# A small pool opened early and first place for the first pair's first tile in two SwiGLU networks of a decoder layer; the second network's first weights written down earlier

## The chip, the cores and the metric

The kernel runs on one core of one Trainium2 chip. The metric is the device time of one execution in microseconds (us). TensorE is the matmul engine, VectorE (DVE) and ScalarE (ACT) and GpSimd (POOL) do the elementwise work, and SyncE's queue (SP) issues most of the transfers.

## The reference

One decoder layer for 1024 prompt tokens and 8 x 4 sample tokens, 1056 in all, with model width 1024:

```
h = rms_norm(x) * (1 + scale) + shift
x = x + 0.5 * gate * swiglu(h)          # first network, D_FF = 2816
h = rms_norm(x) * (1 + scale) + shift
x = x + gate * (concat(gdn(h), mla(h)) @ w_out)      # the mixer
h = rms_norm(x) * (1 + scale) + shift
x = x + 0.5 * gate * swiglu(h)          # second network
...
def swiglu_ffn(h, wi, wo):
    gate, up = jnp.split(h @ wi, 2, axis=-1)
    return (jax.nn.silu(gate) * up) @ wo
```

Shift, scale and gate come from a conditioning vector per sequence (ada_w). All is in fp32.

## The kernel before, in words

**Data.** The 1056 tokens are four blocks of 264 (BW), features on partitions. Blocks 0 and 1 are the first pair (p = 0), blocks 2 and 3 the second. An fp32 product is made of three matmuls of rounded high and low halves (`mm3`, lines 127 to 129); `halve` (369 and 370) makes such halves: a cast on ScalarE, a subtraction on VectorE or GpSimd.

**Up projection.** `ffn_up` goes over 22 tiles of 128 features. Each tile and pair is a 2 x 2 product in Strassen's manner: seven products (PRODUCTS) of one form of the input (B11, T3, T2, B21, T1, T4, B22) with one form of the weights (A11, S3, S2, A12, S1, A22, S4), 12 matmuls each, summed in three PSUM banks X, Y, Z of that pair. `ffn_weights` makes the weight forms from two loads of 512 KB, g and u. `ffn_pair` writes the products and what takes them out of the banks: after B11 a copy s1 (487), after T2 the sums u2 and u3 (476), after T1 and T4 the two halves of cc, after B21 and B22 the Silu sg, at the end cc = sg * cc and its store (502). A bank is written again only after it has been taken out: B21 adds to X after s1, T1 needs Y after u2, T4 adds to Z after u3, B22 adds to Y after cc's half. Tile 0 uses the order B11, B21, T3, T2, T1, T4, B22 and writes the first pair in whole, then the second.

**Input forms.** `norm_squares` sums the squares of a block on ScalarE (nsq, 312) and VectorE or GpSimd (nacc, 315 and 319). `norm_sums` sums over partitions on TensorE (ss, 334) and takes the inverse root in nine small operations on VectorE (336 and 707 to 711). `norm_rows` spreads the root over the partitions on TensorE (rb, 347). `chain` then scales (354, 359, 361, 365), forms the differences (405) and halves the seven forms of a pair. Block 0 and 2 give B11 and B21; the rest of a pair's forms need its second block.

**Around the change.** In the first network the four chains run after the first conditioning products. In the second, `mixer_out` writes the output product: for two pairs of blocks, eight column tiles of w_out, 24 matmuls for each block and tile; the last two column tiles of the second pair are loaded and split by `split` (108 and 111) and multiplied block by block, so that block 2 is finished and normed before block 3. `then` starts a block's chain and is stepped on between products.

**Order of the work.** A planner takes the program as written, with a rank for each instruction from its place. Whenever an engine is free in the planner's own time line, it gives it the ready instruction of the lowest rank; the result is a fixed order for each engine's queue, which the chip keeps. `high_priority(n)` moves instructions n places ahead, `later(n)` n places back (LATE holds these numbers). Memory is a stack of pools; a tile of a pool that lies over an older pool is ordered only after the last use of the older one. The up projection's pool (t1, t2) lies over the norm's pool (tn, tn2) and over the residents x0 to x3, which also stage the chains of blocks 2 and 3. Its banks X, Y, Z lie over those of the output products.

**Weight buffers.** `wsp` has eight buffers of 4 KB per partition for halves of weights, `wraw` three for raw weights. The slots hi0 to hi3 and lo0 to lo3 hold the halves of the mixer's output and later the forms.

Of the kernel before, what the change touches and what calls it, by code (L numbers as in the profile page):

```python
# [8 lines left out]
F32 = mybir.dt.float32  # L9
# [8 lines left out]
P = 128  # L18
# [46 lines left out]
AHEAD = 1500  # L65


LATE = (100, 150, 110, 30, 110)


def f(ap):
# [13 lines left out]
class Kernel:  # L85
# [218 lines left out]
    def norm_squares(self, b, tp, k=0, n=KT, eng=None):  # L304

        nc = self.nc
        x = self.xb[b]
        eng = eng or nc.gpsimd
        for k in range(k, k + n, 2):
            m = min(n, 2)  # L310
            sq = tp.tile([P, 2, BW], F32, tag="nsq", name="nsq", bufs=2)
            nc.scalar.activation(sq[:, :m], x[:, k:k + m, :], AF.Square)
            if k == 0:
                self.nacc[b] = acc = tp.tile([P, BW], F32, tag="nacc", name="nacc", bufs=NB)
                eng.tensor_tensor(out=acc, in0=sq[:, 0], in1=sq[:, 1], op=ALU.add)
            else:
                acc = self.nacc[b]
                for j in range(m):
                    eng.tensor_tensor(out=acc, in0=acc, in1=sq[:, j], op=ALU.add)
# [5 lines left out]
    def norm_sums(self, blocks, tp, ps, late=0):  # L325

        nc = self.nc
        W = BW // 4
        ss = ps.tile([P, 512], F32, tag="C", name="ss")
        n = 4 * len(blocks)  # L330
        for at, b in enumerate(blocks):
            with self.later(late):
                for q in range(4):
                    nc.tensor.matmul(ss[:W, 4 * at + q:4 * at + q + 1], self.nacc[b][:, q * W:(q + 1) * W], self.ones, start=True, stop=True)
        v, r, t = (tp.tile([W, 4 * NB], F32, tag=n, name=n, bufs=3)[:, 0:n_] for n, n_ in (("nv", n), ("nr", n), ("nq", n)))
        nc.vector.tensor_scalar(v, ss[:W, 0:n], 1.0 / D, EPS, ALU.mult, ALU.add)
        self.rsqrt(r, v, t)
        for at, b in enumerate(blocks):
            self.nr[b] = r[:, 4 * at:4 * at + 4]

# [128 lines left out]
        part("S4", A12, nc.vector)  # L469
        return W  # L470

    def ffn_pair(self, p, W, dst, tp, ps, products):

        nc = self.nc
        T = lambda n: tp.tile([P, self.ffn_tiles[n][0]], F32, tag=f"{n}{p}", name=n, bufs=self.ffn_tiles[n][1])
        tt = lambda out, a, b, op=ALU.add: nc.vector.tensor_tensor(out=out, in0=a, in1=b, op=op)
        sg, cc = T("sg"), T("cc")
        B, F = {}, self.forms[p]
        for x, w, bank, add in products:
            if not add:  # L480
                B[bank] = ps.tile([P, 512], F32, tag=f"{bank}{p}", name="p" + bank)[:, 0:BW]
            for k in range(4):
                self.mm3(B[bank], W[w][:, 0, k], W[w][:, 1, k], F[x][:, 0, k], F[x][:, 1, k], k == 0 and not add, k == 3 and (add or x == "T2"),
                         skip_group_check=True)
            if x == "B11":
                s1 = T("s1")
                nc.scalar.copy(s1, B["X"])
            elif x == "T2":
                u2, u3 = T("u2"), T("u3")
                tt(u2, s1, B["Y"])  # L490
                tt(u3, u2, B["Z"])
            elif x == "B21":
                nc.scalar.activation(sg[:, :BW], B["X"], AF.Silu)
            elif x == "T1":
                tt(cc[:, BW:], u3, B["Y"])
            elif x == "T4":
                tt(cc[:, :BW], u2, B["Z"])
            elif x == "B22":
                tt(u3, u2, B["Y"])
                nc.scalar.activation(sg[:, BW:], u3, AF.Silu)  # L500
                tt(cc, sg, cc, ALU.mult)
                nc.sync.dma_start(out=dst[:, 2 * BW * p:2 * BW * p + 2 * BW], in_=cc)
            yield

    def ffn_up(self, wi, tp, ps, hook=lambda us: None, first=None):


        nf = wi.shape[1] // 2 // P

        self.ffn_tiles = {"cc": (2 * BW, 2), "sg": (2 * BW, 1), "u3": (BW, 1), "u2": (BW, 1), "s1": (BW, 1)}  # L510
        for p in range(2):
            for n, (w, bufs) in self.ffn_tiles.items():
                tp.tile([P, w], F32, tag=f"{n}{p}", name=n, bufs=bufs)
        for ff in range(nf):
            W = first if first and ff == 0 else self.ffn_weights(wi, ff, tp)
            order = PRODUCTS if ff else (PRODUCTS[0], PRODUCTS[3], *PRODUCTS[1:3], *PRODUCTS[4:])
            pairs = [self.ffn_pair(p, W, self.act_d[ff], tp, ps, order) for p in range(2)]
            for g in pairs if ff in (0, nf - 1) else [zip(*pairs)]:
                for _ in g:
                    hook(1.45 if g in pairs else 2.9)  # L520

    def ffn_down(self, wo, mgate, tp, ap, ps, each, load):

# [158 lines left out]
    def hook(self):  # L682

        done = object()
        for g in list(self.active):
            if next(g, done) is done:
                self.active.remove(g)
# [1369 lines left out]
                    for _ in smp:  # L2057
                        pass

    def mixer_out(self, tp, tn, ps, then):  # L2060


        nc, wo = self.nc, self.i["w_out"][0]
        parts = [self.mix_split(b) for b in range(NB)]

        def product(b, d, w):
            po = ps.tile([P, 512], F32, tag="B", name="po")
            for k in range(KT):
                self.mm3(po[:, :BW], w[0][:, k, :], w[1][:, k, :], parts[b][0][:, k, :], parts[b][1][:, k, :], k == 0, k == KT - 1)
            self.residual(b, d, 5, po, tp)  # L2070
        load = lambda d: self.split(self.load_cols(wo, d * P, P), (KT, P))
        side = iter(())
        for h in range(2):
            pair = (2 * h, 2 * h + 1)
            for d in range(KT - 2 * h):
                w = load(d)
                for b in pair:
                    product(b, d, w)
                    if d % 2:
                        self.norm_squares(b, tn, d - 1, 2, nc.gpsimd)  # L2080
                    next(side, None)
            if h == 0:
                self.norm_sums(pair, tn, ps)
                side = then(0, then(1, iter(())))
        ws = [load(d) for d in range(KT - 2, KT)]
        for b in pair:
            for n, w in enumerate(ws):
                product(b, KT - 2 + n, w)
                next(side, None)
                self.norm_squares(b, tn, KT - 2 + n, 1, nc.vector)  # L2090
            self.norm_sums([b], tn, ps, LATE[2] if b % 2 else 0)
            side = then(b, side)
        for _ in side:
            pass
# [19 lines left out]
def body(tc, ins, outs):  # L2114
# [15 lines left out]
    def pool(name, **kw):  # L2130
        return tc.tile_pool(reuse_waits="tile", name=name, bufs=1, **kw)

    with k.ctx:
        k.setup()
        k.dram()
        with k.weights():
            with k.extra():
                with k.residents(), ExitStack() as pse, pool("tn") as tn, pool("t0") as tp:
                    ps = banks(pse, "ps0", **DOWN)
                    k.small_vectors(ps, "C")  # L2140
# [13 lines left out]
                with ExitStack() as pse, pool("t1") as tp, pool("tk") as tk:  # L2154
                    ps = banks(pse, "ps1", **UP)

                    def background():
                        k.key_tables(tk, ps, "C")
                        yield from k.ada(2, 1, tk, ps, "C")
                        for m in (3, 5, 7):  # L2160
                            yield from k.ada(m, 2, tk, ps, "C")
                        raw = k.bcast_load(tk, ins["gdn_a_log"][0], H, "g_alog")
                        nc.scalar.activation(k.alog, raw, AF.Exp)
                    bg, credit = background(), [0.0]

                    def hook(us):
                        credit[0] += us
                        while credit[0] > 0:
                            next(bg, None)
                            credit[0] -= PACE  # L2170
                    k.ffn_up(ins["ffn1_wi"][0], tp, ps, hook, first)
                    run(bg)
            with k.residents(), ExitStack() as pse, pool("a1", side="right") as a0, pool("b1", side="right") as a1, pool("tn1") as tn:
                ps = banks(pse, "ps2", **DOWN)
# [28 lines left out]
        with heads:  # L2203
            k.mixer_heads()
        with k.weights():
            with k.extra():
                with k.residents(), ExitStack() as pse, pool("tn2") as tn:
                    ps = banks(pse, "ps3", **DOWN)
                    k.load_xb(k.x1_d, nc.sync)
# [1 line left out]
                    def then(b, side):  # L2211
# [3 lines left out]
                        k.store_xb(k.x2_d, b)  # L2215
                        if not b:
                            yield from side
                    k.mixer_out(tn, tn, ps, then)
                with ExitStack() as pse, pool("t2") as tp:
                    k.ffn_up(ins["ffn2_wi"][0], tp, banks(pse, "ps4", **UP))  # L2220
            with k.residents(), ExitStack() as pse, pool("a2", side="right") as a0, pool("b2", side="right") as a1, pool("tn3") as tn:
                ps = banks(pse, "ps5", **DOWN)

# [34 lines left out]
```

## Time and profile before

| | us |
|---|---|
| median of 3 runs | 2859.01 (2853.66 to 2862.34) |
| the profiled execution | 2863.72 |
| its span, first to last instruction | 2861.9 |
| TensorE busy | 2673.6 (93%) |
| VectorE busy | 1766.6 (62%) |
| ScalarE busy | 1074.2 (38%) |
| GpSimd busy | 1083.2 (38%) |
| mean granted clock of TensorE | 0.955 of full |

A row of the timeline has the start, the time taken, the engine, the line of the kernel, the operation, out<-in with the shapes, how many instructions it stands for, and in brackets the idle time of the engine before it and what ended that. A row of a stretch has its bounds and length, then for TensorE's matmuls, its weight loads, VectorE, ScalarE and GpSimd the busy time and the number of instructions, then the granted clock, the DMA share and GB/s. The first network's up projection starts at 50.34 us, the second's at 2112.23.

### The profile page before, as it was taken

The numbers are of one execution on the slowest core, as the hardware profiler recorded it, in microseconds if no ns is written. First come the engines' busy times: TensorE is split into PE (matmuls) and PEld (weight loads), VectorE is DVE, ScalarE is ACT, GpSimd is POOL, SyncE is SP. The second block draws the span as 40 slices with busy tenths as digits, with TensorE's granted clock in tenths as the row PEclk, the third lists the DMA queues.
The fourth block names the chain that finished last, engine by engine and source line by source line (L and its number), as shares of the span: only waits on it lengthen the run. The fifth ranks groups of instructions, "written<-read, shape, count | busy, mean of one in ns | idle before, by whom it ended". The sixth has DMA issues, their size and how long they took to land.

```text
span 2861.9 us, 53475 instructions
## 1 busy us (share of the span) xinstructions
PE 2673.6 (93%) x21536; PEld 2462.5 (86%) x21536; DVE 1766.6 (62%) x3490; ACT 1074.2 (38%) x2005; POOL 1083.2 (38%) x1032
## 2 busy tenths in 40 slices
PE   4999999989999897799999988998979999999999
PEld 3888989989999787787877866776979999999999
DVE  7644445465574688847767677777585555546555
ACT  5322223211144443324656664543443333322111
POOL 0222222233352555544434466452433333323331
PEclk7999999999999998898999998987979999999999
DMA  7554353243232473432212144222522222224322
GB/s 272 154 163 134 120 162 105 81 161 106 76 109 77 149 206 117 141 110 78 63 42 58 49 96 114 83 64 53 188 82 82 76 87 71 90 82 167 98 76 69
DMA packets 339490, 308.35 MB, mean 108 GB/s; under 512 B 93865, under 2 KB 282017, under 8 KB 336171
## 3 DMA queue, kind: packets, MB, share of 16 engines
q1 hardware_dynamic: 304837, 246.32, 28.4%
q10 hardware_dynamic: 28262, 37.64, 4.1%
q0 software_dynamic: 6144, 20.98, 2.3%
q8 instruction: 169, 2.77, 0.4%
q14 instruction: 78, 0.64, 0.1%
HBM read 229.29 MB, written 75.59 MB: 107 GB/s over the span
## 4 chain that ended last, share of the span: by engine, by line
PE 42%; DVE 8%; issue 5%; POOL 4%; DMA 2%; ACT 1%; SPq 0%; ACTq 0%; POOLq 0%; DVEq 0%
PE po L128 4%; PE po L129 4%; PE po L127 4%; PE pY L127 2%; PE pY L128 2%; PE pY L129 2%; PE kraw L127 2%; PE pX L127 2%; PE pX L128 2%; PE pX L129 1%; PE pZ L127 1%; PE pZ L129 1%; PE pZ L128 1%; PE kraw L129 1%; PE kraw L128 1%
## 5 line engine op out<-in xcount | busy, mean ns | idle before, releaser
L127 PE MATMUL po<-act,whi 128*128 128x264 f32 x1408 | 402.4, 286 | 6.4 <-DVE x L435 4.7
L129 PE MATMUL po<-act,wlo 128*128 128x264 f32 x1408 | 403.2, 286 | 0.0
L128 PE MATMUL po<-act,whi 128*128 128x264 f32 x1408 | 402.0, 286 | 0.0
L435 DVE SCALAR_TENSOR_TENSOR x<-po,modT,x 128x264 f32<-128x264 f32 (+1 forms) x416 | 195.2, 480 | 238.8 <-PE po L129 238.3
L127 PEld LDWEIGHTS po<-act,whi 128*128 128x128 f32 x1408 | 266.8, 189 | 7.1 <-DVE x L435 4.9
L129 PEld LDWEIGHTS po<-act,wlo 128*128 128x128 f32 x1408 | 266.1, 189 | 0.0
L128 PEld LDWEIGHTS po<-act,whi 128*128 128x128 f32 x1408 | 265.9, 189 | 0.0
L370 POOL TENSOR_TENSOR A<-wg,A 128x512 fp32r<-128x512 f32 x84 | 111.0, 1321 | 372.1 <-ACT A L369 372.1
L127 PE MATMUL pp<-hhi,whi 128*128 128x264 f32 (+1 forms) x768 | 223.9, 292 | 4.5 <-DVE nt L354 3.6
L128 PE MATMUL pp<-hlo,whi 128*128 128x264 f32 (+1 forms) x768 | 223.7, 291 | 0.0
L129 PE MATMUL pp<-hhi,wlo 128*128 128x264 f32 (+1 forms) x768 | 221.8, 289 | 0.0
L2001 DVE TENSOR_REDUCE kss<-ksq 128x8 f32<-128x512 f32 x256 | 173.1, 681 | 69.7 <-ACT ksq L2000 67.7
L127 PE MATMUL pX<-B,A 128*128 128x264 f32 x704 | 203.9, 290 | 10.6 <-ACT B L369 9.7
L111 POOL TENSOR_TENSOR wlo<-wraw,whi 128x1024 fp32r<-128x1024 f32 x39 | 97.7, 2510 | 305.2 <-ACT whi L108 305.2
L2000 ACT ACTIVATE ksq<-kraw 128x512 f32<-128x512 f32 x256 | 152.1, 598 | 162.1 <-PE kraw L129 122.2
L128 PE MATMUL pX<-B,A 128*128 128x264 f32 x704 | 202.9, 288 | 8.9 <-DVE B L370 8.9
L128 PE MATMUL pY<-T,S 128*128 128x264 f32 x704 | 200.7, 285 | 1.6 <-DVE T L370 1.5
L129 PE MATMUL pX<-B,A 128*128 128x264 f32 x704 | 201.6, 286 | 0.0
L127 PE MATMUL pY<-T,S 128*128 128x264 f32 x704 | 200.3, 285 | 0.0
L129 PE MATMUL pY<-T,S 128*128 128x264 f32 x704 | 200.2, 284 | 0.0
L1700 POOL TENSOR_TENSOR plo<-pf,phi 128x512 fp32r<-128x512 f32 (+1 forms) x96 | 97.1, 1017 | 187.4 <-ACT phi L1699 169.7
L108 ACT CAST whi<-wraw 128x1024 fp32r<-128x1024 f32 x60 | 61.8, 1048 | 253.6 <-PE po L128 234.1
(538 smaller groups left out, 8305.1 us busy)
## 6 DMA issues: line engine op xcount, KB each, us to landing
adaw<-ada_w SPq DMA_DIRECT2D x72, 512.0 KB
wraw<-ffn_wi SPq DMA_DIRECT2D x46, 512.0 KB
act_d<-cc SPq DMA_DIRECT2D x88, 264.0 KB
wraw<-ffn_wo SPq DMA_DIRECT2D x44, 512.0 KB
wg<-ffn_wi SPq DMA_DIRECT2D x42, 512.0 KB
araw<-act_d ACTq DMA_DIRECT2D x160, 132.0 KB
x_d<-x SPq DMA_DIRECT2D x12, 1056.0 KB
wraw<-w_in SPq DMA_DIRECT2D x23, 512.0 KB
```

What stands on the lines that cost most here:

```text
L108: nc.scalar.copy(hi, raw)
L111: eng.tensor_tensor(out=lo, in0=raw, in1=f(hi), op=ALU.subtract)
L127: nc.tensor.matmul(out, whi, ahi, start=first, stop=False, **kw)
L128: nc.tensor.matmul(out, whi, alo, start=False, stop=False, **kw)
L129: nc.tensor.matmul(out, wlo, ahi, start=False, stop=last, **kw)
L370: eng.tensor_tensor(out=lo, in0=src, in1=f(hi), op=ALU.subtract)
L435: nc.vector.scalar_tensor_tensor(out=x[:, d, :n], in0=ps[:, :n], scalar=self.modT[:, m, d, 0:1], in1=x[:, d, :n], op0=ALU.mult, op1=ALU.add)
L1700: nc.gpsimd.tensor_tensor(out=lo[:, off:], in0=pf[:, off:], in1=f(hi[:, off:]), op=ALU.subtract)
L2000: nc.scalar.activation(sq, kr, AF.Square)
L2001: nc.vector.tensor_reduce(out=ss[:, (j * 4 + m) * H:(j * 4 + m + 1) * H], in_=sq.rearrange("p (h d) -> p h d", h=H), axis=AX.X, op=ALU.add)
```

## The change

- Two pools, `tf` and `tf2`, are opened below the norm's pool and the residents. In the first pair's first tile (`early`) s1, u3 and the first half c1 of the product's other factor are tiles there, and u2 is written over s1. sg and cc stay in the up projection's pool. The last multiplication is written in two halves there.
- That pair's tile is moved 300 places ahead (SOON), in both networks, with the background steps that its hook starts.
- The operations of the inverse root in `norm_sums` are moved 300 places ahead, everywhere.
- nacc has two buffers for four. The first pair's tiles in the up projection's pool are laid out in the reverse order.
- LATE's fourth number, which holds back block 2's row spread in the second network, is 12 for 30.
- In `mixer_out` the last column tile of w_out goes to the slot lo1, with its low half on VectorE, and the second network's first weights (`ahead`) are written before the last four products.

```diff
-LATE = (100, 150, 110, 30, 110)
+LATE = (100, 150, 110, 12, 110)
+SOON = 300
...
-                self.nacc[b] = acc = tp.tile([P, BW], F32, tag="nacc", name="nacc", bufs=NB)
+                self.nacc[b] = acc = tp.tile([P, BW], F32, tag="nacc", name="nacc", bufs=2)
...
-        nc.vector.tensor_scalar(v, ss[:W, 0:n], 1.0 / D, EPS, ALU.mult, ALU.add)
-        self.rsqrt(r, v, t)
+        with self.tc.high_priority(SOON):
+            nc.vector.tensor_scalar(v, ss[:W, 0:n], 1.0 / D, EPS, ALU.mult, ALU.add)
+            self.rsqrt(r, v, t)
...
-    def ffn_pair(self, p, W, dst, tp, ps, products):
+    def ffn_pair(self, p, W, dst, tp, ps, products, early=None):
...
+        E = lambda n: early.tile([P, BW], F32, name=n) if early else T(n)
+        c1 = E("c1") if early else cc[:, BW:]
...
-                s1 = T("s1")
+                s1 = E("s1")
...
-                u2, u3 = T("u2"), T("u3")
+                u2, u3 = s1 if early else T("u2"), E("u3")
...
-                tt(cc[:, BW:], u3, B["Y"])
+                tt(c1, u3, B["Y"])
...
-                tt(cc, sg, cc, ALU.mult)
+                if early:
+                    tt(cc[:, BW:], sg[:, BW:], c1, ALU.mult)
+                    tt(cc[:, :BW], sg[:, :BW], cc[:, :BW], ALU.mult)
+                else:
+                    tt(cc, sg, cc, ALU.mult)
...
-            for n, (w, bufs) in self.ffn_tiles.items():
+            for n, (w, bufs) in list(self.ffn_tiles.items())[::1 if p else -1]:
...
-                for _ in g:
-                    hook(1.45 if g in pairs else 2.9)
+                with self.tc.high_priority(SOON if ff == 0 and g is pairs[0] else 0):
+                    for _ in g:
+                        hook(1.45 if g in pairs else 2.9)
...
-        ws = [load(d) for d in range(KT - 2, KT)]
+        ws = [load(KT - 2)]
+        raw, t = self.load_cols(wo, (KT - 1) * P, P), self.slot("lo1", [P, KT * BW], F32R, "wlast")
+        ws.append([t[:, n * D:n * D + D].rearrange("p (k c) -> p k c", k=KT) for n in range(2)])
+        self.halve(*ws[1], raw, nc.vector)
+        ahead()
...
-            with k.extra():
+            with k.extra(), pool("tf2") as early:
...
-                    k.mixer_out(tn, tn, ps, then)
+                    ready = []
+                    k.mixer_out(tn, tn, ps, then, lambda: ready.append(k.ffn_weights(ins["ffn2_wi"][0], 0, None)))
...
-                    k.ffn_up(ins["ffn2_wi"][0], tp, banks(pse, "ps4", **UP))
+                    k.ffn_up(ins["ffn2_wi"][0], tp, banks(pse, "ps4", **UP), first=ready[0], early=early)
```

More of the change, by code (lines that the diff above doesn't have):

```diff
@@ L500, in ffn_pair, with ffn_up @@
                 nc.scalar.activation(sg[:, BW:], u3, AF.Silu)
-                tt(cc, sg, cc, ALU.mult)
+                if early:
[3 more added lines that the diff above has]
+                    tt(cc, sg, cc, ALU.mult)
                 nc.sync.dma_start(out=dst[:, 2 * BW * p:2 * BW * p + 2 * BW], in_=cc)
             yield
-    def ffn_up(self, wi, tp, ps, hook=lambda us: None, first=None):
+    def ffn_up(self, wi, tp, ps, hook=lambda us: None, first=None, early=None):
         nf = wi.shape[1] // 2 // P
@@ L516, in ffn_up @@
             order = PRODUCTS if ff else (PRODUCTS[0], PRODUCTS[3], *PRODUCTS[1:3], *PRODUCTS[4:])
-            pairs = [self.ffn_pair(p, W, self.act_d[ff], tp, ps, order) for p in range(2)]
+            pairs = [self.ffn_pair(p, W, self.act_d[ff], tp, ps, order, early if ff + p == 0 else None) for p in range(2)]
             for g in pairs if ff in (0, nf - 1) else [zip(*pairs)]:
-                for _ in g:
-                    hook(1.45 if g in pairs else 2.9)
+                with self.tc.high_priority(SOON if ff == 0 and g is pairs[0] else 0):
+                    for _ in g:
+                        hook(1.45 if g in pairs else 2.9)
     def ffn_down(self, wo, mgate, tp, ap, ps, each, load):
@@ L2058, in mixer_heads, with mixer_out @@
                         pass
-    def mixer_out(self, tp, tn, ps, then):
+    def mixer_out(self, tp, tn, ps, then, ahead):
         nc, wo = self.nc, self.i["w_out"][0]
@@ L2136, in body @@
         with k.weights():
-            with k.extra():
+            with k.extra(), pool("tf") as early:
                 with k.residents(), ExitStack() as pse, pool("tn") as tn, pool("t0") as tp:
@@ L2170, in hook @@
                             credit[0] -= PACE
-                    k.ffn_up(ins["ffn1_wi"][0], tp, ps, hook, first)
+                    k.ffn_up(ins["ffn1_wi"][0], tp, ps, hook, first, early)
                     run(bg)
@@ L2205, in body @@
         with k.weights():
-            with k.extra():
+            with k.extra(), pool("tf2") as early:
                 with k.residents(), ExitStack() as pse, pool("tn2") as tn:
```

## The prediction

> **What bounds the kernel now.** I read the page first (spans and shares, then the chain), then the timeline of TensorE at the start of each up projection, then VectorE and ScalarE there.
>
> ```profile
> span 2861.9 us, 53475 instructions
> PE 2673.6 (93%) x21536; PEld 2462.5 (86%) x21536; DVE 1766.6 (62%) x3490; ACT 1074.2 (38%) x2005; POOL 1083.2 (38%) x1032
> PE 42%; DVE 8%; issue 5%; POOL 4%; DMA 2%; ACT 1%; SPq 0%; ACTq 0%; POOLq 0%; DVEq 0%
> 50.30:85.30 35.00, 16.01 (x72) 14.11 (x72) 35.00 (x38) 23.88 (x35) 4.08 (x3) 0.62 0.13 35
> 85.30:102.90 17.60, 16.05 (x123) 13.64 (x123) 11.58 (x19) 8.08 (x14) 7.26 (x5) 1.00 0.64 206
> 2080.00:2103.50 23.50, 23.48 (x195) 23.26 (x193) 23.50 (x28) 11.46 (x16) 17.32 (x10) 1.00 0.16 46
> 2112.20:2142.60 30.40, 16.28 (x90) 14.97 (x89) 24.68 (x45) 14.78 (x23) 0.00 (x0) 0.61 0.20 70
> ```
>
> TensorE (second column of the stretches) bounds the whole, except at the two places the change touches: the 35 us after the first network's first product and the 30 us after the last output product, where it is busy 16 us each at a granted clock of 0.6. In the first, VectorE (fourth column) is busy throughout; it makes the normalised forms.
>
> First network, TensorE's waits (in brackets) and what ScalarE and VectorE do beside:
>
> ```profile
> 63.09 0.59 PE L127 MATMUL pX<-B,A 128*128 128x264 f32 x1 [4.48 <-ACT B L369]
> 74.48 0.59 PE L127 MATMUL pZ<-T,S 128*128 128x264 f32 x1 [4.54 <-ACT T L369]
> 80.45 0.39 PE L128 MATMUL pY<-T,S 128*128 128x264 f32 x1
> 82.79 0.39 PE L128 MATMUL pY<-T,S 128*128 128x264 f32 x1 [0.73 <-DVE T L370]
> 85.34 0.39 PE L127 MATMUL pX<-B,A 128*128 128x264 f32 x1 [0.94 <-ACT s L487]
> 86.66 0.28 PE L128 MATMUL pX<-B,A 128*128 128x264 f32 x1
> 86.78 0.28 PE L129 MATMUL pX<-B,A 128*128 128x264 f32 x1
> 101.33 0.39 PE L127 MATMUL pY<-B,S 128*128 128x264 f32 x1 [1.27 <-DVE cc L476]
> 84.91 0.37 ACT L487 COPY s<-pX 128x264 f32<-128x264 f32 x1
> 61.73 1.24 DVE L370 TENSOR_TENSOR B<-st,B 128x1056 fp32r<-128x1056 f32 x1
> 81.48 4.81 DVE L370 TENSOR_TENSOR T<-st,T 128x1056 fp32r<-128x1056 f32 x4
> 86.21 0.42 DVE L476 TENSOR_TENSOR u<-s,pY 128x264 f32<-128x264 f32 x1
> ```
>
> Each pair may run three products (12 matmuls each, into banks X, Z, Y) before something must leave a bank. The first copy out (s, 84.91) stands on ScalarE behind all the form casts, although TensorE had left that product behind by 63.09. So TensorE does 72 matmuls in 35 us and starts the other 96 of the first tile at 85.34. At full rate a matmul takes 0.12 us (starts 86.66, 86.78).
>
> Second network:
>
> ```profile
> 2108.08 1.06 PE L334 MATMUL ss<-ones,nacc 128*66 128x1 f32 x8 [4.60 <-DVE nacc L319]
> 2112.01 0.42 PE L129 MATMUL po<-mhi,wlo 128*128 128x264 f32 x1
> 2112.23 0.42 PE L127 MATMUL pX<-B,A 128*128 128x264 f32 x1
> 2116.76 0.40 PE L347 MATMUL rb<-ident,nr 66*128 66x66 f32 x4
> 2121.74 0.59 PE L127 MATMUL pX<-B,A 128*128 128x264 f32 x1 [3.20 <-ACT B L369]
> 2134.43 0.59 PE L127 MATMUL pZ<-T,S 128*128 128x264 f32 x1 [8.17 <-ACT T L369]
> 2140.07 0.59 PE L128 MATMUL pY<-T,S 128*128 128x264 f32 x1 [0.74 <-DVE T L370]
> 2153.97 0.28 PE L127 MATMUL pX<-B,A 128*128 128x264 f32 x1
> 2117.19 2.42 DVE L354 TENSOR_TENSOR st<-x,rb 128x1056 f32<-128x1056 f32 x2 [2.41 <-PE rb L347]
> 2119.53 0.15 DVE L336 TENSOR_SCALAR nv<-ss 66x4 f32<-66x4 f32 x1
> 2124.90 0.16 DVE L711 SCALAR_TENSOR_TENSOR nr<-nq,nr 66x4 f32<-66x4 f32 x1
> 859.01 0.15 DVE L336 TENSOR_SCALAR nv<-ss 66x4 f32<-66x4 f32 x1
> 860.93 0.16 DVE L711 SCALAR_TENSOR_TENSOR nr<-nq,nr 66x4 f32<-66x4 f32 x1
> 2139.86 0.37 ACT L487 COPY s<-pX 128x264 f32<-128x264 f32 x1
> ```
>
> The last output product ends at 2112.2. The forms of the second pair (blocks 2 and 3) are ready only at 2140; the 8.17 us wait is block 3's chain: sums, root, row broadcast, scaling, differences, halves. Again the copy out comes after the last form (2139.86), and 11 + 96 matmuls of tile 0 remain.
>
> **The change part by part.**
>
> *Early pool and priority, first network.* The s, u, c tiles of the first pair's first tile move from a pool opened over the normalisation's memory to one that exists beforehand, so the copy can be ordered among the forms. The first pair can then do all 84 matmuls as its forms come. Its B21 form is there at 63 (row 61.73 + 1.24), so 12 matmuls x 0.12 = 1.5 us go into the waits before 74.48. T1, T4 and B22 follow its T2 (80.45) and can fill the waits 0.73, 0.94 and 1.27, 2.9 us. Against it: u2, u3 and c1 now stand among the halves, 3 x 0.42 = 1.3 us (row 86.21), so the last half ends near 87.6 instead of 86.3; T2, T1, T4, B22 of the first and T2 of the second pair (60 x 0.12 = 7.3 us from 80.45, to 87.7) cover this. New waits: u2 may queue behind one 1.24 us half before T1 can take its bank, about 1.0, and the second pair's first copy comes after the last form, about 0.6. Sum: 1.5 + 2.9 - 1.6 = 2.8 us gained. Bounds: 4.4 with no new wait; 0.2 if only B21 moves and the evictions are paid (1.5 - 1.3).
>
> *The same, second network.* The banks X, Y, Z lie over the output products' banks, so the first pair still starts behind the last output product. Its 48 further matmuls fit into the 3.20 and 8.17 us waits, where they cost nothing: behind 2140 there remain 11 + 48 instead of 11 + 96, a gain of 48 x 0.12 = 5.8 us. What moves 2140 itself:
> - The root's nine small operations get priority. For block 3 they took 2119.53 to 2125.06, 5.5 us, between other work; alone, at 859.01, 2.1 us. Gain 3.4.
> - Block 2's row broadcast (2116.76) now has the first pair ahead of it. Until that pair first waits (T1 for u2), 48 matmuls go: 11 at the slow 0.22 us (starts 2112.01, 2112.23) and 37 at 0.12 are 6.9 us, to 2119.1: a loss of 2.4. Bounds: at best the broadcast slips through and VectorE's 2.41 us wait is saved as well, which is also all that the smaller LATE (30 to 12) can give; at worst all 84 go first (11 x 0.22 + 73 x 0.12 = 11.2, to 2123.4), a loss of 6.7.
> - u2 and u3 on VectorE ahead of block 3's forms: 2 x 0.42 = 0.8 (bounds 0.8 and, with c1 and the second u3, 1.7).
>
> Together 3.4 - 2.4 - 0.8 = +0.2. I take 5.8 + 0.2 = 6.0; bounds 5.8 + 3.4 + 2.4 - 0.8 = 10.8 and 5.8 + 3.4 - 6.7 - 1.7 = 0.8.
>
> *Weights ahead.* Tile 0's weights: two loads, seven ScalarE casts, six VectorE and five GpSimd operations, now written before the last products. They are not late today: the loads are out before 2090.4; and the first casts run at 2090.7.
>
> ```profile
> 2073.57 16.84 SPq L117 DMA_DIRECT2D wraw<-ffn_wi  x3
> 2090.71 0.60 ACT L369 CAST A<-wraw 128x512 fp32r<-128x512 f32 x1
> 2086.60 3.41 POOL L111 TENSOR_TENSOR wlo<-wraw,whi 128x1024 fp32r<-128x1024 f32 x1
> 2081.80 1.21 DVE L111 TENSOR_TENSOR wlo<-wraw,whi 128x1024 fp32r<-128x1024 f32 x1
> ```
>
> So I cost the gain at nothing. The last output weight's low half goes from GpSimd (3.41 us) to VectorE (1.21 us), which is 23.50 of 23.50 us busy there, and TensorE waits 4.60 us for its squares at 2108: at most 1.2 us lost, at best as much gained by fewer operations on GpSimd beside. I take 0. That weight lies in the slot of a second-pair form written at 2120, after its last reader (2112): no wait.
>
> *At nothing:* two nacc buffers for four (a block's sum is taken before the second next block's squares); the multiply in two halves and the reversed tile order (VectorE is busy 11.58 of 17.60 us after 85.3). The background's loads traced inside the priority use memory that frees with the last form, as now.
>
> Sum: 2.8 + 6.0 = 8.8 us. The profiled execution took 2863.72 us (its span and 1.8 around it), so 2854.9; it lies 4.7 above the median of the runs shown, 2859.01, and against that the forecast is 2850. A measurement of this kernel tells about 0.3%, 8.6 us, from no change (the three runs span 8.7), so 2850.4 is the border.
>
> **A rule beside the rows.** After the wait of 4.60 us matmuls start 0.22 us apart until 2114.4, 6 us, then 0.12:
>
> ```profile
> 2114.58 0.28 PE L129 MATMUL pX<-B,A 128*128 128x264 f32 x1
> 2114.70 0.28 PE L127 MATMUL pZ<-T,S 128*128 128x264 f32 x1
> ```
>
> So the second pair's last 60 matmuls, after a wait that I expect to stay over 5 us, pay 24 x 0.1 = 2.4 us (24 starts of 0.22 make 5.3 us), as they do now; this is in neither sum as a change. The Trainium skill ("TensorE: Matmul & The Clock Gate", "What's actually happening") says that the clock halves after an idle window of about 3.4 us and is released after a busy one of about 3.4 us. The rows agree on the idle side and show a longer release. By that rule a wait cut below 3.4 us would gain these 2.4 us as well: part of the second case below.
>
> **The rivals.**
> - *The chain shortens too:* the broadcast slips through the first pair's gaps, and the root's 3.4 us and part of the 2.4 us stay. For it: nothing but matmuls stands between. Against it: the priority puts 84 of them ahead. 4 + 9 = 13 us, and with the clock 15: 2844 to 2847.
> - *The gain is half taken back:* the broadcast waits for nearly all 84, or tile 1's weights end last. Their load starts when the last form frees memory (in the second network A11's low half ends at 2147.4 and tile 1 starts at 2153.97: room for 6.6 us, less what the forms' end slips).
>
> ```profile
> 2146.07 1.30 POOL L370 TENSOR_TENSOR A<-wg,A 128x512 fp32r<-128x512 f32 x1 [35.42 <-ACT A L369]
> ```
>
>  That leaves 3 to 5 us: 2854 to 2856.
> - *Nothing happens:* the copies out stay behind the forms, as the order is made by a planner: 2859.
> - *Slower:* evictions placed early wait in VectorE's and ScalarE's queues, with the forms behind them, for products that run at the slow clock. Four per network (s, u2, c1, u3) x a product at 12 x 0.22 = 2.6 us is 10.6; twice 21, less the 9 gained, 12: 2871. It decides once more than two of the four per network stand ahead of their product's end. Against it: in 50 to 85 the order on every engine follows readiness closely.
>
> **How the numbers follow.** Forecast 0.40 (own range 2846 to 2853, its middle at the border), shorter chain 0.25, half taken back 0.24, nothing 0.04, slower 0.07. Faster: 0.25 + 0.26 of the forecast's 0.40 = 0.51; slower 0.07; within 0.3%: the rest, 0.42. The range goes from both best bounds (4.4 + 10.8, 2843.8) to just past no change, 2860; the slower case and part of the extremes stay out.
>
> **What would show it.** Right: the first copy out near 59 and near 2115, over 100 matmuls in the 35 us and 30 us stretches, the root of block 3 in under 3 us, waits behind 85 gone. Wrong: block 2's broadcast more than 5 us after the last output product, a longer 4.60 us wait, or VectorE idle behind an eviction among the halves.

## The result, and the profile after

| kernel | median of the runs, us | runs | ratio to before | 95% interval |
|---|---|---|---|---|
| before | 2859.49 (2853.66 to 2862.34) | 4 | 1 | |
| changed | 2843.47 (2840.76 to 2844.36) | 4 | 0.9945 | 0.9928 to 0.9962 |

The change gains 16.0 us; the forecast was 9, so 2850. The changed kernel's profiled execution took 2843.14 us, 20.6 less than that of before, which lay 4.2 above its own median. Its page, and its stretches of the same lengths as those shown of before, counted from the first product of the first network, up to the end of the output products, and from the first product of the second network:

```profile
span 2841.1 us, 53324 instructions
PE 2671.2 (94%) x21536; PEld 2462.6 (87%) x21536; DVE 1733.8 (61%) x3493; ACT 1071.7 (38%) x2005; POOL 1089.1 (38%) x1031
49.97:84.97 35.00, 19.86 (x92) 17.76 (x93) 35.00 (x39) 24.21 (x37) 4.09 (x3) 0.62 0.20 59
84.97:102.57 17.60, 17.60 (x140) 15.41 (x139) 12.84 (x23) 9.46 (x17) 8.29 (x6) 1.00 0.45 142
2067.20:2090.70 23.50, 23.50 (x196) 23.50 (x195) 23.50 (x31) 13.38 (x22) 14.72 (x10) 1.00 0.12 35
2099.66:2130.06 30.40, 17.97 (x130) 16.82 (x129) 24.64 (x51) 14.66 (x22) 0.00 (x0) 0.78 0.15 54
```

TensorE's busy time has hardly moved (2673.6 to 2671.2): the gain is idle time of TensorE. The first stretch holds 92 records of matmuls for 72, the next 140 for 123, the last 130 for 90.

Both programs run 21536 matmuls, so the two traces can be laid beside each other by count: when does the N-th matmul start? The difference (after less before), in us:

| place (number of the matmul) | difference | won or lost since the row above |
|---|---|---|
| first product of the first network | -0.3 | |
| tile 0 of its up projection done (400) | -4.9 | -4.5 |
| end of its up projection (4000) | -3.7 | +1.2 |
| in its down projection (4500) | -10.2 | **-6.5** |
| first product of the second network | -12.6 | -2.4 |
| tile 1 of its up projection (16000) | -16.2 | -3.6 |
| late in its up projection (19000) | -14.4 | +1.8 |
| in its down projection (20000) | -20.2 | **-5.9** |
| end | -20.8 | -0.6 |

The two starts, on which the forecast rests, gave 8.1. The 2.4 is inside what the mixer varies (below). The two rows in bold are more than that, and the forecast has nothing at those places. They lie where an up projection hands over to its down projection. TensorE's waits there in the kernel before:

```profile
577.78 0.39 PE L127 MATMUL pY<-B,S 128*128 128x264 f32 x1 [1.51 <-DVE cc L476]
588.55 0.47 PE L127 MATMUL po<-act,whi 128*128 128x264 f32 x1 [4.67 <-DVE x L435]
2582.84 0.59 PE L127 MATMUL pY<-B,S 128*128 128x264 f32 x1 [3.39 <-DVE cc L476]
```

A wait costs more than its length there. Behind the 3.39, matmuls start 0.22 us apart and no longer 0.12, for 26 starts (granted clock 0.50 from 2582.8 to 2586), which is 2.6 us more; behind the 4.67 it is 15 starts, 1.5 us. The first of them at 2583:

```profile
2583.22 0.42 PE L128 MATMUL pY<-B,S 128*128 128x264 f32 x1
2583.45 0.42 PE L129 MATMUL pY<-B,S 128*128 128x264 f32 x1
```

So 3.39 + 2.6 = 6.0 us stand beside the 5.9 won at the second handover, and 1.51 + 4.67 + 1.5 = 7.7, less what is left of waits, beside the 6.5 of the first. Who holds the 4.67, ScalarE's queue and then VectorE's, in the kernel before:

```profile
584.35 2.54 ACTq L551 DMA_DIRECT2D araw<-act_d  x3
586.93 0.42 ACT L500 ACTIVATE sg<-u 128x264 f32<-128x264 f32 x1 [4.10 <-DMA araw<-act_d]
587.38 0.71 DVE L476 TENSOR_TENSOR cc<-sg,cc 128x528 f32<-128x528 f32 x1 [3.30 <-ACT sg L500]
588.01 2.08 DVE L435 SCALAR_TENSOR_TENSOR x<-po,modT,x 128x264 f32<-128x264 f32 x5
```

Read it upwards. The matmul at 588.55 needs a bank; VectorE empties it at 588.01, behind its multiply; the multiply waits 3.30 us for the activation of the last tile; and that stands on ScalarE behind three loads of `araw`, which are issued from ScalarE's queue for the down projection. In the changed kernel the same places, TensorE and ScalarE:

```profile
575.76 0.39 PE L129 MATMUL po<-act,whi 128*128 128x264 f32 x1 [0.90 <-DVE act L372]
577.58 0.42 ACT L505 ACTIVATE sg<-u 128x264 f32<-128x264 f32 x1 [0.93 <-DMA x<-x_d]
2558.54 0.39 PE L128 MATMUL pY<-T,S 128*128 128x264 f32 x1 [0.60 <-DVE u L479]
```

No wait above 0.9 us is left at either handover.

### The profile page after: what moved, and what is told of

It is laid out like the page before. It is cut to its first block, busy times and chain, and to the rows that moved or that the text cites. A ratio compares the mean times of both kernels' runs of the same rounds, so it can differ in the third digit from the quotient of the medians.

```text
span 2841.1 us, 53324 instructions
## 1 busy us (share of the span) xinstructions
PE 2671.2 (94%) x21536; PEld 2462.6 (87%) x21536; DVE 1733.8 (61%) x3493; ACT 1071.7 (38%) x2005; POOL 1089.1 (38%) x1031
## 4 chain that ended last, share of the span: by engine, by line
PE 42%; DVE 7%; POOL 6%; issue 5%; DMA 2%; ACT 1%; SPq 0%; DVEq 0%; POOLq 0%; ACTq 0%
PE po L129 4%; PE po L128 4%; PE po L130 4%; PE pY L128 2%; PE pY L129 2%; PE pY L130 2%; POOL gt L102 2%; PE pX L128 2%; PE pX L129 2%; PE pX L130 1%; PE pZ L128 1%; PE pZ L129 1%; PE pZ L130 1%; PE kraw L128 1%; PE kraw L130 1%
## 5 line engine op out<-in xcount | busy, mean ns | idle before, releaser
L479 DVE TENSOR_TENSOR cc<-u,pY 128x264 f32<-128x264 f32 x86 | 36.7, 426 | 207.5 <-PE pY L130 203.6
```

## The experiments

Each ratio is to runs of the kernel before on the same chip, whose medians there were 2867.46, 2853.58, 2858.54 and 2852.97 us; "by the count" means the differences of the table above.

**Where the handover gain comes from.** The diff's last line of `ffn_up` puts every pair of every tile into a priority block; only for the first pair of tile 0 is its offset 300, elsewhere it is 0. In the planner the block restores its counter of priority at its end: inside, the counter of the changed kernel runs from 347 to 539 for the products of tile 1, and stands at 347 again behind it. So in the changed kernel the tiles begin at 327, 347, 367 ..., 20 apart (the weights alone), where without the block each tile's products count too, and a later tile ranks behind an earlier one. Theory A: this alone gives the handovers, since the last two tiles are now interleaved and both first activations come ahead of the loads of `araw`. Theory B: the reversed order of the first pair's tiles does it. Theory C: it follows from the earlier start.

`only_wrapper`, an edit of the kernel before:

```
-                for _ in g:
-                    hook(...)
+                with self.tc.high_priority(0):
+                    for _ in g:
+                        hook(...)
```

> The kernel before with one edit: each pair's loop stands in a priority block of offset 0. Theory A (the block sets the planner's priority counter back when it ends, so that no tile ranks behind the tiles traced before it, and this alone gives the two gains of about 6 us where an up projection hands over to its down projection): the waits of 4.67 us near 588 and of 3.39 us near 2583 are gone, the first copies out stay where they are (near 84.8 and 2140), the time falls by 10 to 13 us from 2859.5, to 2847 to 2850. Theory B (the reversed tile order gives the two gains) and theory C (the earlier start re-phases the rest): an offset of 0 is nothing, 2859.5 within 4, waits as before.

Measured: 0.9981 (0.9966 to 0.9995), 5.2 us less between the medians, half of what A said. By the count of matmuls it won 6.0 us at the first handover and 3.1 at the second. Of the 1.51 and 4.67 us at the first this is left, and 1.05 us at 597:

```profile
582.75 0.39 PE L128 MATMUL po<-act,whi 128*128 128x264 f32 x1 [0.91 <-DVE act L370]
```

But it lost 5.4 us by matmul 330, about half of it in one new wait for tile 1's weights, which the tiles' mixing lets TensorE meet earlier, and 1.4 us in the 14 matmuls that start 0.22 us apart behind it:

```profile
92.23 0.43 PE L127 MATMUL pX<-B,A 128*128 128x264 f32 x1 [2.72 <-ACT A L369]
```

`no_wrapper`, an edit of the changed kernel:

```
-                with self.tc.high_priority(SOON if ff == 0 and g is pairs[0] else 0):
+                with self.tc.high_priority(SOON) if ff == 0 and g is pairs[0] else ExitStack():
```

> The changed kernel, with the priority block around the first pair of each network alone and no block of offset 0 around any other pair. Theory A: the waits at both handovers come back (4.7 and 3.4 us), the fast starts stay (first copies near 63 and 2102 by the changed kernel's clock of events), so 12 of the gain are lost and 4 to 9 us stay: 2851 to 2856. Theories B and C: reversed tiles and early start are still there, so 2843.5 within 3 and no waits at the handovers.

Measured: 0.9969 (0.9955 to 0.9984): some 9 us of gain stay. The starts stay fast, the handovers are back (nothing won by the count at the second, 1.2 lost at the first). The blocks are needed, as A says, and the earlier start alone does not do it, so C falls:

```profile
572.66 0.39 PE L128 MATMUL pY<-B,S 128*128 128x264 f32 x1 [1.74 <-DVE cc L479]
584.03 0.59 PE L128 MATMUL po<-act,whi 128*128 128x264 f32 x1 [5.26 <-DVE x L437]
2579.71 0.59 PE L128 MATMUL pY<-B,S 128*128 128x264 f32 x1 [3.41 <-DVE cc L479]
```

`only_tiles`, an edit of the kernel before:

```
-            for n, (w, bufs) in self.ffn_tiles.items():
+            for n, (w, bufs) in list(self.ffn_tiles.items())[::1 if p else -1]:
```

> The kernel before with one edit: the first pair's tiles reserve their memory in reversed order. Theory B: 10 to 13 us faster than 2859.5, the 4.67 us and 3.39 us waits gone. Theory A: no change, 2859.5 within 3. The prediction on record costed this edit at nothing as well.

Measured: 1.0005 (0.9992 to 1.0018). B falls. Its handovers, whose waits are divided otherwise and come to 9.65 us for 9.57:

```profile
577.51 0.39 PE L127 MATMUL pY<-B,S 128*128 128x264 f32 x1 [2.18 <-DVE cc L476]
587.64 0.39 PE L127 MATMUL po<-act,whi 128*128 128x264 f32 x1 [2.48 <-DVE x L435]
2585.15 0.59 PE L127 MATMUL pY<-B,S 128*128 128x264 f32 x1 [4.99 <-DVE cc L476]
```

`only_wrap_last2`, an edit of the kernel before that asks whether the loss of `only_wrapper` comes from the tiles between:

```
+                with self.tc.high_priority(0) if ff >= nf - 2 else ExitStack():
```

> The kernel before with one edit: blocks of offset 0 around the last two tiles of each up projection, none elsewhere. It is left open by the kernel with the blocks everywhere, which won the handovers (6.0 and 3.1 us by its trace) and lost 3 us on the way to each. If the loss there is the mixing of all the other tiles: the starts are the old ones (second pair's T3 at 22.0 us behind the second network's first product, with 47 matmuls ahead of it), no loss at matmul 330, both handover waits under 1.5 us, and 9 to 12 us under the kernel before, ratio 0.996 to 0.997. Rival: the block as such loses some 3 us per network wherever it stands: 0.998 again.

Measured: 0.9940 (0.9919 to 0.9962), 15.6 us less between the medians: one line in the kernel before measures about what the whole change does. By its trace the handovers won 6.7 and 3.2, the second network's start was the old one (T3 at 21.5 us behind the first product, 48 matmuls ahead of it), and the loss at matmul 330 is gone. The median is more than the 9.9 of the handovers; the interval, in us 11 to 23, begins just above. What the rest is stays open: the mixer between the networks took 1149.7 us in this trace and 1161.2 in that of before, but over the fourteen traces it varies from 1149.7 to 1166.9, and for one program in two executions (the changed kernel) it was 1159.9 and 1155.4.

```profile
576.21 0.39 PE L128 MATMUL po<-act,whi 128*128 128x264 f32 x1 [0.91 <-DVE act L370]
2561.76 0.39 PE L128 MATMUL po<-act,whi 128*128 128x264 f32 x1 [0.79 <-DVE act L370]
```

**What the starts owe to the pool and to the priority.** `no_pair_priority` is the changed kernel with offset 0 for the first pair too:

```
-                with self.tc.high_priority(SOON if ff == 0 and g is pairs[0] else 0):
+                with self.tc.high_priority(0):
```

> The changed kernel with offset 0 in place of 300 for the first pair (the early pool and the blocks stay). If the early pool alone lets the copy out go ahead (it was held by memory): first copy still near 63.5 in the first network, and 2843.5 within 3. If the priority does it: the first copy returns to the neighbourhood of 80 to 85, the two starts lose about 9 us, 2852. In the second network the priority is what puts 48 matmuls of the first pair ahead of block 2's row broadcast, so without it the broadcast comes earlier (about 4.5 us after the last output product in place of 6.3) and this network may gain 1 to 2 us more.

Measured: 0.9938 (0.9921 to 0.9955), as the changed kernel. The memory had held the copy out, not its rank: with the pool alone it is early. ScalarE in the first network, then TensorE's row broadcasts and the wait for T3 in the second, whose first product starts at 2109.89:

```profile
63.97 0.36 ACT L492 COPY s<-pX 128x264 f32<-128x264 f32 x1
```

```profile
2114.92 0.40 PE L349 MATMUL rb<-ident,nr 66*128 66x66 f32 x4
2124.83 0.42 PE L349 MATMUL rb<-ident,nr 66*128 66x66 f32 x4 [0.32 <-DVE nr L723]
2133.42 0.59 PE L128 MATMUL pZ<-T,S 128*128 128x264 f32 x1 [8.17 <-ACT T L371]
```

Block 2's broadcast comes 5.0 us behind that first product, for 6.3 with the priority. The converse shows in the plan: with the priority alone, in the kernel before, the planned order has the first network's first two copies out at the places in ScalarE's order that they have without it.

`pool_only` is the changed kernel without any of the new priorities, blocks and weights ahead:

```
-                with self.tc.high_priority(SOON if ff == 0 and g is pairs[0] else 0):
+                with ExitStack():
-LATE = (100, 150, 110, 12, 110)
+LATE = (100, 150, 110, 30, 110)
... (root without its block, mixer_out and the second network's weights as before)
```

> The kernel before with the early pool in both networks, two nacc buffers, the multiply of the first pair in halves and the reversed tiles, but without any priority, without blocks of offset 0 and without the weights made ahead. If the gain is the sum of two starts (early pool) and two handovers (counter set back): both starts quicken as in the changed kernel (48 more matmuls ahead of the second pair's T3 in the second network; 3 to 5 us in each network), the handover waits stay (4.7 and 3.4 us as before): 6 to 9 us under the kernel before, ratio 0.997 to 0.998. Rival: without the priority the copies out slip back behind the forms: no change.

Measured: 0.9979 (0.9962 to 0.9996), 6 us by the ratio. By the count it won 4.5 in the first start and 4.0 in the second, nothing to speak of at the handovers:

```profile
580.60 0.59 PE L128 MATMUL po<-act,whi 128*128 128x264 f32 x1 [4.81 <-DVE x L437]
2574.86 0.59 PE L128 MATMUL pY<-B,S 128*128 128x264 f32 x1 [3.43 <-DVE cc L479]
```

**The root and the weights ahead**, on one chip with the changed kernel itself.

> The changed kernel once more, to stand beside the next three on the same chip. 0.9945 of the kernel before, within 0.0015 (some 16 us).

Measured: 2840.17 us, 0.9950 (0.9934 to 0.9966).

`no_root_priority`:

```
-        with self.tc.high_priority(SOON):
+        with self.tc.high_priority(0):
             nc.vector.tensor_scalar(v, ss[:W, 0:n], 1.0 / D, EPS, ALU.mult, ALU.add)
```

> The changed kernel with offset 0 in place of 300 for the nine small operations of the root. By the prediction on record they gain 3.4 us in the second network: the time would rise by 3.4 over the changed kernel's, and the root of block 3 (first to last of its operations) would take longer than the 6.3 us that the changed kernel shows. Rival, from that 6.3 (5.5 before): the priority moves a handful of VectorE operations past their neighbours and shortens nothing, because they still alternate with the first pair's u and c: the changed kernel's time within 2 us.

Measured: 2840.11 us, 0.9953 (0.9936 to 0.9970): nothing that can be measured. Block 3's root takes 6.4 us on VectorE, first and last operation:

```profile
2106.15 0.15 DVE L338 TENSOR_SCALAR nv<-ss 66x4 f32<-66x4 f32 x1
2112.40 0.16 DVE L723 SCALAR_TENSOR_TENSOR nr<-nq,nr 66x4 f32<-66x4 f32 x1
```

`no_ahead`, the last output weight and tile 0's weights as in the kernel before:

```
-        ws = [load(KT - 2)]
-        ...
-        ahead()
+        ws = [load(d) for d in range(KT - 2, KT)]
```

> The changed kernel without the weights made ahead: the last output weight and tile 0's weights of the second network are made where they were before. The prediction on record has 0 within 1.2 us. Rival: the 8.17 us wait for the second pair's T2 and the 3.79 us wait for block 2's squares depend on how much VectorE and ScalarE still have to do behind the last output product, and the weights' 7 casts and 6 differences are part of it: 2 to 4 us slower than the changed kernel, with the first product of the second network later behind the last output product, or a wait for W there.

Measured: 2841.68 us, 0.9947 (0.9926 to 0.9967): no difference clear of the noise. The wait for block 2's squares is 0.8 us longer. From the first product to matmul 16000 it takes 63.1 us for 64.2 in the changed kernel beside it, but that does not show that the 0.8 comes back: behind the wait for T3 only 10 matmuls start 0.22 us apart in this trace, for 33 beside it, and the 62 matmuls from there take 12.6 us for 14.1. That is the clock's phase (see the end) and not the edit:

```profile
2096.32 0.96 PE L335 MATMUL ss<-ones,nacc 128*66 128x1 f32 x8 [4.58 <-DVE nacc L320]
```

**Is there a better version?** `wrap_last2` is `no_pair_priority` with the block around the last two tiles only:

```
-                with self.tc.high_priority(0):
+                with self.tc.high_priority(0) if ff >= nf - 2 else ExitStack():
```

> The changed kernel with offset 0 for the first pair (it needed no priority) and the block of offset 0 only around the last two tiles of each up projection; the other tiles stand in none. If the set-back counter helps only where the up projection ends, and in its middle lets tiles mix to no use (the kernel with the blocks alone lost 5 to 7 us there against the kernel before, the changed kernel some 2 in each network): both handover gains stay (no wait over 1.5 us at 576 and 2567) and the time is 2 to 4 us under the changed kernel's. Rival: the counter must be set back over the whole projection for the last tiles to mix: the handover waits return, 8 to 12 us slower than the changed kernel.

> Once more, to stand beside the next one: 0.994 of the kernel before, within 0.002.

Measured: 2838.47 us, 0.9943 (0.9924 to 0.9962), and again 2835.87 us, 0.9926 (0.9907 to 0.9944). The handovers stay won (5.5 and 5.0 us by the first trace), so the last two tiles are enough. The gain of 2 to 4 us expected over the changed kernel was 1.7 between the medians of one chip; the intervals overlap, and it is not shown.

`root_first` goes on from there and takes the two halves out from among the root's operations:

```
-LATE = (100, 150, 110, 12, 110)
+LATE = (100, 150, -300, 12, -300)
+        if b == 2 and mscale == 7:
+            for n in ("B11", "B21"):
+                with self.tc.issue_after(self.root.ins):
+                    done(n, n)
+                yield
+            return
```

> The kernel with blocks around the last two tiles alone, and in the second network block 3's sums and row broadcast ahead of other work (300 in place of 110 behind), and the halves of block 2's B11 and B21 issued on VectorE behind the root of block 3, so that these two pieces of 1.24 us no longer stand among the root's nine operations. If block 3's chain sets the end of the wait of 8.17 us: its row broadcast comes 2 to 3 us earlier than 14.4 us behind the first product, the wait for T3 ends 2 to 3 us earlier than 22.95, and the second pair's 12 products on B11 and B21 move behind that: 1 to 2.5 us less than the kernel beside it. Rival: VectorE's work as a whole sets the end (its pieces are only reordered), so the last form and what follows end at the same time: within 1 us.

Measured: 2834.63 us, 0.9923 (0.9904 to 0.9942), 1.2 less than the kernel beside it and inside the interval. VectorE's root and TensorE's row broadcast and wait for T3 in `root_first` (first product at 2092.18), then TensorE of the kernel beside it (first product at 2095.57):

```profile
2097.11 0.16 DVE L338 TENSOR_SCALAR nv<-ss 66x4 f32<-66x4 f32 x1 [2.60 <-PE ss L335]
2103.38 0.16 DVE L729 SCALAR_TENSOR_TENSOR nr<-nq,nr 66x4 f32<-66x4 f32 x1
```

```profile
2105.04 0.40 PE L349 MATMUL rb<-ident,nr 66*128 66x66 f32 x4
2114.26 0.59 PE L128 MATMUL pZ<-T,S 128*128 128x264 f32 x1 [7.42 <-ACT T L371]
```

```profile
2109.68 0.42 PE L349 MATMUL rb<-ident,nr 66*128 66x66 f32 x4 [0.32 <-DVE nr L723]
2118.27 0.59 PE L128 MATMUL pZ<-T,S 128*128 128x264 f32 x1 [8.17 <-ACT T L371]
```

The root ends 2.6 us earlier behind the first product (11.4 for 14.0), the broadcast 1.2 (it then stands behind products on TensorE), the wait for T3 ends 0.6 earlier. So of 2.6 us taken out of the chain, 0.6 reached its end. Up to matmul 16000 both kernels win the same, 6.4 and 6.6 us, but the two traces differ in the clock behind that wait: 26 matmuls start 0.22 us apart in `root_first` and 10 in the kernel beside it, and the 62 matmuls from there take 13.5 us for 12.6. That the 0.6 is lost again is therefore not shown. A gain of 1.2 us, with these intervals, fits both the expectation (1 to 2.5 us) and the rival (within 1), by which VectorE's work as a whole sets the end; the run does not decide between them.

## Why the prediction was right, and where it was not

The time was on the forecast's side, but 6.5 us under it: outside its own range of 2846 to 2853 and at the lower end of the whole range, whose two best bounds gave 2843.8. Two errors of opposite sign and one missing term stand behind it. That the time still fell at the range's edge is luck: of the 15.2 us of its two best bounds the starts gave 8.1, and what filled the distance is a gain at places that the forecast does not name.

**First network, +2.8 forecast, 4.5 measured** (3.3 at the projection's end; what took 1.2 back in between stays open, since the changed kernel's second trace lost nothing there, and `root_first`, which has no blocks around those tiles, 1.3). The size is that of the bound without new waits, 4.4: the 0.94 and 1.27 us behind 85 are gone, only the 0.73 is left, at 82.41, and of the deducted 1.6 us of new waits one of 0.66 at 64.01 shows, ahead of the wait for T3, where it costs nothing. TensorE's waits from 62 on, first rows and last, and ScalarE's first copy out:

```profile
62.76 0.59 PE L128 MATMUL pX<-B,A 128*128 128x264 f32 x1 [4.47 <-ACT B L371]
64.01 0.59 PE L128 MATMUL pX<-B,A 128*128 128x264 f32 x1 [0.66 <-ACT s L492]
73.00 0.43 PE L128 MATMUL pZ<-T,S 128*128 128x264 f32 x1 [3.33 <-ACT T L371]
82.41 0.39 PE L129 MATMUL pY<-T,S 128*128 128x264 f32 x1 [0.73 <-DVE T L372]
```

```profile
63.58 0.38 ACT L492 COPY s<-pX 128x264 f32<-128x264 f32 x1
```

The copy is at 63.6, not near 59, and the stretch has 92 matmuls, not over 100: T1, T4 and B22 came later than thought, and all the same in time. Two of the signs that the prediction named for this network were so missed although the gain came.

**Second network, +6.0 forecast, 3.6 measured.** Its terms, each against the first product at 2099.68 (2112.23 before):

```profile
2097.05 0.86 PE L335 MATMUL ss<-ones,nacc 128*66 128x1 f32 x8 [3.79 <-DVE nacc L320]
2105.96 0.40 PE L349 MATMUL rb<-ident,nr 66*128 66x66 f32 x4
2115.18 0.42 PE L349 MATMUL rb<-ident,nr 66*128 66x66 f32 x4 [0.58 <-DVE nr L723]
2123.76 0.59 PE L128 MATMUL pZ<-T,S 128*128 128x264 f32 x1 [8.17 <-ACT T L371]
```

```profile
2101.82 0.38 ACT L492 COPY s<-pX 128x264 f32<-128x264 f32 x1 [0.54 <-PE pX L130]
```

```profile
2104.78 0.43 DVE L479 TENSOR_TENSOR s<-s,pY 128x264 f32<-128x264 f32 x1 [2.78 <-PE pY L130]
2108.73 0.15 DVE L338 TENSOR_SCALAR nv<-ss 66x4 f32<-66x4 f32 x1
2114.87 0.16 DVE L723 SCALAR_TENSOR_TENSOR nr<-nq,nr 66x4 f32<-66x4 f32 x1
```

- The 48 matmuls: exact. Ahead of the second pair's T3 stand 96 matmuls of the products for 48, so 48 fewer behind it, the forecast's 5.8 us. The copy out comes 2.3 us behind the first product.
- Block 2's row broadcast, -2.4: held. It comes 6.3 us behind the last output product for 4.5, a loss of 1.8, after the 48 matmuls counted on. This was to be a sign of error if over 5, wrongly: the sum itself had 6.9.
- The root's +3.4: the step that failed within this sum. It took 6.3 us, 0.8 more than before. The 2.1 us of the row at 859 were those of a VectorE with nothing else to do; here its operations (eleven in the trace, not nine) each wait for the one before, and VectorE starts another piece of up to 1.25 us in between. A priority ranks what is ready and does not hold VectorE free. In `no_root_priority` this term is 0 within the noise, and in `root_first` 2.6 us out of the root shortened the wait for T3 by 0.6.
- u2 and u3, -0.8: the size is right, the pieces are others. u2 and u3 ran at 2104.78 and 2105.25, ahead of block 2's broadcast, and VectorE stood still for 2.78 us before u2, one of the prediction's signs of error; the broadcast was not there either, so it cost little. c1 and the second u3 (0.41 us at 2108.80, 0.43 at 2111.28) stand among the root's operations, and they are its 0.8.

In sum 5.8 less the 1.9 us by which T3 came later (24.1 us behind the first product for 22.2) is 3.9, for 3.6 by the count.

**Weights ahead, 0 forecast, nothing measurable** (`no_ahead`); the wait for the squares shrank by 0.8, inside the 1.2 allowed. The reversed tiles, costed at nothing, are nothing (`only_tiles`). So is the smaller LATE: with 30 in place of 12 the planned program of the changed kernel is the same on every engine.

**The missing term, 12.4 us in the trace** (6.5 + 5.9; the same blocks lose 1.8 on the way there in the second network, where the traces of kernels with blocks around the middle tiles lose 1.6 to 2.7 and those without 0.0). The list of what costs nothing left out the block of offset 0 around all other pairs: I read it as no change, and looked for the change's effects only at the two places that it names. The block sets the planner's counter back and reorders both up projections to their ends. The waits that it removes were in the trace of before: 1.51 + 4.67 in the first network and 3.39 in the second, and the slow clock behind them, are on no line of the prediction. The two starts themselves came to 4.5 + 3.6 = 8.1 for the 8.8 of the forecast: a sum that was right by luck, of two parts that were off by 1.7 upwards and 2.4 downwards.

**The rivals.** That the chain would shorten (2844 to 2847) was nearest in time and wrong in its reason: the chain grew by 1.9 us. Of the others none happened; nothing queued behind an early eviction cost more than the 2.78 us above.

## What to carry to other kernels

Where a block, a scope or a helper is put around a whole loop and only one turn of the loop is meant, ask what it does in all the others: offset 0 was not nothing, since the block sets a counter back, and one such line, around the last two tiles alone, measured 15.6 us, of which its trace shows 9.9 at the handovers. Before costing an edit, list the waits of TensorE over 1 us in the whole trace and not only those at the named place; an edit that reorders may meet any of them. Count with such a wait the matmuls behind it that start 0.22 us apart: here 1.5 and 2.6 us for waits of 4.67 and 3.39. The price of a chain of small operations on a busy engine is read from a place where that engine is as busy, not from one where it idles.

## What the chip showed beyond that

After the wait for block 2's squares (3.8 to 4.6 us in all traces) the matmuls start 0.22 us apart and later 0.12. Before, that took 6 us; in the changed kernel it ended after 3.7, at 2100.76 (TensorE's rows there):

```profile
2100.56 0.37 PE L129 MATMUL pX<-B,A 128*128 128x264 f32 x1
2100.76 0.29 PE L130 MATMUL pX<-B,A 128*128 128x264 f32 x1
2100.89 0.29 PE L128 MATMUL pX<-B,A 128*128 128x264 f32 x1
```

In twelve of the fourteen traces it took 3.7 to 7.1 us (the changed kernel 3.7 and, once more, 3.9); in `no_pair_priority` and `no_wrapper` the slow starts began only 1.2 and 0.8 us behind the end of the wait. The Trainium skill ("TensorE: Matmul & The Clock Gate", "What's actually happening") says that the window by which the clock is released runs free, so that the point depends on where in it the work begins; the spread agrees with that, and is far wider than the 0.5 us each way that it names. At 0.1 us lost per matmul the 26 slow starts of the longest cost 2.6 us and the 11 of the changed kernel 1.1, so this moves what stands behind them: block 2's row broadcast, behind the same 48 matmuls, comes 6.3 us after the first product in the changed kernel and 7.1 and 7.6 in `no_ahead` and `no_root_priority`.

Behind the wait for T3 the spread is wider: 10 to 34 matmuls start 0.22 us apart there (31 before, 33 in the changed kernel), 2.4 us at 0.1 each. Two kernels whose traces differ by less than that at this place are not told apart by one trace each. A wait need not be long for it: in `only_tiles`, after the wait of 2.18 us at 577.51, the granted clock was 1.00 for 1.4 us more and then 0.52 for 3.4 us. So the prediction's step that a wait cut below 3.4 us would be spared the slow starts is not borne out; the 3.39 above was followed by 26 of them.
